# Expert lookups in float16 on VectorE alone, shared phase products, and the gathered rows of the first layer moved behind its U products

## The chip, the cores and the metric

The kernel runs on one core of a Trainium2 chip. The metric is the device time of one execution in microseconds; of the kernel before, three runs gave 2900.38, 2909.81 and 2911.41 us (median 2909.81). A difference is measured between runs of both kernels on one chip.

The engines are named as the profile names them: PE multiplies matrices (PEld is its weight load), DVE is VectorE, ACT is ScalarE, POOL is GpSimd, SP is SyncE, which here only issues DMAs. Each engine works through its own list of instructions in order.

## The reference, cut to what matters

Two layers over 256 latent tokens and 256 context tokens, 1024 features wide. Layer 0 mixes tokens with a gated MLP, layer 1 with a diagonal state-space scan; each is followed by an expert network that looks its experts up by two half keys. Only the latent tokens are given out. The lookup, for each token and each of 8 heads:

```
s_half, i_half = lax.top_k(s, 16)                 # best 16 of 128 keys, for each half
cand = s_half[:, :, 0, :, None] + s_half[:, :, 1, None, :]
top_s, top_c = lax.top_k(cand.reshape(..., 256), 16)
k1 = take_along_axis(i_half[:, :, 0], top_c // 16)   # the lookup of the first half
k2 = take_along_axis(i_half[:, :, 1], top_c % 16)    # and of the second
ids = k1 * 128 + k2
g = softmax(top_s)
act = gelu(einsum("nd,nhkd->nhk", hb, u_tab[ids]))
out = einsum("nhk,nhkd->nd", g * act, v_tab[ids])
```

The scan of layer 1 needs, for each of its states, the powers 1, z, z^2, ... of a rotation z (64 of them, as real and imaginary parts). The program calls them phases.

## The kernel before, in words

**The expert network, dense for most tokens.** For 384 of layer 0's 512 tokens (the latent ones and half of the context) and for layer 1's 256 tokens the kernel doesn't fetch experts by row: it multiplies all tokens with all 16384 experts, in 128 blocks of 128, and weights the products with a gate matrix that is zero where a token did not pick the expert. `front` (a U product) loads a block of U, splits it into a high and a low part (ACT copies `uh`, DVE subtracts to get `ul`), runs 24 matmuls and takes the gelu. `back` loads a block of V, multiplies the activations with the gates (`w`), splits both (`wh`, `wl`, `vh`, `vl`) and runs 18 matmuls (12 in layer 1) into PSUM. The first 62 (layer 0) and 66 (layer 1) U products stand ahead of the first V product; most of their activations go to DRAM and come back later (`act_d`, `actr`). The other U products stand among the V products.

**What is done beside the first U products.** The top-16 searches of the routing and the lookups (`route`, per tile of 128 tokens, in two groups of four heads each), then the gates (`gate_units`): DVE makes `eq` and two products `o` for every 8 tokens, PE multiplies them. The generators of this work are called a step at a time between the U products (`during`, `spread`). In layer 0 there are four tiles of tokens: the three dense ones and a fourth, routed first, whose 128 context tokens are the gathered ones.

**The lookup in the code before.** For each half, DVE takes the high or low four bits of the candidate's number (`pi`), casts them to float32 (`pf`), compares each with 0 to 15 (`oh`, line 504: 128 x 1024 elements, the last index being the 16 places), POOL multiplies that with the key numbers (line 506) and DVE sums over the 16 places (line 507). There are 12 groups of two halves: 8 in layer 0, 4 in layer 1.

**The gathered rows.** For the fourth tile the kernel fetches rows of U and V by index with an indirect DMA on POOL's queue (line 596), 128 + 128 of them, each 128 tokens x 1024, four buffers (`ROWS`) in turn. DVE takes a dot product with each U row (line 606, `gscr`) and adds each weighted V row to `acc` (line 619). A unit is two rows. `EARLY0` = 8 units stand among the first U products; of the rest, `MID0` = 18 units are spread over the first 56 V products and the others up to 97% of the work that follows (`cut`, `GEND`).

**The phases.** `phase_units` builds the powers for 16 groups of states at a time by doubling: with z^1 to z^k known it multiplies them by z^k. A complex product is done by 6 instructions of DVE (lines 927 to 929, three for the real and three for the imaginary part), in 6 doublings and 4 blocks: 24 times. They stand beside the first V products of layer 0.

**What sets the order.** The program is written as the generators run; then a scheduler with a model of the engines sets the order of each engine's list by that. PE's order in the V products is held as it was written (`manual_schedule`), and the gathers keep theirs. DMAs that load are issued by SP, gathers by POOL, the rest by ACT.

Of the kernel before, what the change touches and what calls it, by code (L numbers as in the profile page):

```python
# [15 lines left out]
OP = mybir.AluOpType  # L16
# [35 lines left out]
ROWS = 4  # L52
EARLY0 = 8
MID0 = 18
# [52 lines left out]
def tile_hybrid(ctx: ExitStack, tc: tile.TileContext, I, out, stop=None):  # L107
# [227 lines left out]
    def gmlp(gw, hh, hl, r, vpump, vdone, upump, mid, pump):  # L335
# [5 lines left out]
        with ExitStack() as st:  # L341
# [106 lines left out]
            with tc.issue_after(ends["out"]):  # L448
# [6 lines left out]
                   allow_small_or_imprecise_dtypes=True)  # L455
    i16 = i128[:, 0:TOPK]

# [13 lines left out]
    def route(pr, S, gates, ids, kk, big={}):  # L471
# [5 lines left out]
        for g in range(2):  # L477
            sv = pr.tile([P, HH, 2, TOPK], F32, name="sv")
            si = pr.tile([P, HH, 2, TOPK], U32, name="si")
            for h in range(HH):  # L480
# [3 lines left out]
                yield 2.5  # L484
            sf = pr.tile([P, HH, 2, TOPK], F32, name="sf")
            nc.vector.tensor_copy(sf, si)
            cand = pr.tile([P, HH, TOPK, TOPK], F32, name="cand", **big)
# [3 lines left out]
            for h in range(HH):  # L491
                scr = pr.tile([P, TOPK * TOPK], F32, name="scr2")
                top16(pr, tv[:, HH * g + h, :], ti[:, h, :], cand[:, h].rearrange("p a b -> p (a b)"), scr)
                yield 2.5
            for half in range(2):
                pi = pr.tile([P, HH, TOPK], U32, name="pi")
                if half == 0:
                    nc.vector.tensor_scalar(pi, ti, 4, None, op0=OP.logical_shift_right)
                else:
                    nc.vector.tensor_scalar(pi, ti, TOPK - 1, None, op0=OP.bitwise_and)  # L500
                pf = pr.tile([P, HH, TOPK], F32, name="pf")
                nc.vector.tensor_copy(pf, pi)
                oh = pr.tile([P, HH, TOPK, TOPK], F32, name="oh", **big)
                nc.vector.tensor_tensor(oh, pf.unsqueeze(3).to_broadcast(full),
                                        i16[:, None, None, :].to_broadcast(full), op=OP.is_equal)
                nc.gpsimd.tensor_tensor(oh, oh, sf[:, :, half, :].unsqueeze(2).to_broadcast(full), op=OP.mult)
                nc.vector.tensor_reduce(kk[half][:, HH * g:HH * g + HH], oh, axis=AX.X, op=OP.add)
                yield 2.5
        if ids is not None:
# [381 lines left out]
    def phase_units(pw):  # L891
# [21 lines left out]
        for g0 in range(0, G, n):  # L913
# [5 lines left out]
            while k < NC_ - 1:  # L919
                m = min(k, NC_ - 1 - k)  # L920
                sh = [P, n, m]
                x, y = ph[:, :, :, 1:m + 1], ph[:, :, :, k:k + 1]
                o = ph[:, :, :, k + 1:k + 1 + m]
                y0, y1 = (y[:, r].to_broadcast(sh) for r in range(2))
                t = pw.tile([P, n, NC_ // 2], F32, name="pht", tag="adasv", bufs=1)[:, :, :m]
                for r, op in ((0, OP.subtract), (1, OP.add)):
                    nc.vector.tensor_tensor(t, x[:, 1], y0 if r else y1, op=OP.mult)
                    nc.vector.tensor_tensor(o[:, r], x[:, 0], y1 if r else y0, op=OP.mult)
                    nc.vector.tensor_tensor(o[:, r], o[:, r], t, op=op)
                    yield  # L930
                k += m
# [303 lines left out]
    def spread(*items):  # L1235

        state = [[g, n, a, b, 0] for g, n, a, b in items]

        def pump(t):
            for s in state:  # L1240
                g, n, a, b, _ = s
                while s[4] < n * min((t - a) / (b - a), 1.0):
                    s[4] += next(g, None) or 1
        return pump

    def layer0():
# [53 lines left out]
        with pool("hx") as ph, pool("hold", side="right") as pk, ExitStack() as hold:  # L1300
# [57 lines left out]
            with pool("de0", 2) as pd, ExitStack() as rs:  # L1358
# [7 lines left out]
                def between():  # L1366
# [6 lines left out]
                    cut = (AHEAD0 - KEEP0) / (2 * KEYS - AHEAD0)  # L1373
                    rest.append(spread((gathers, MID0, 0.0, cut), (gathers, 128 - early - MID0, cut, GEND), (phases, 53, *PW),
                                       (ada, NQ - NS, *AW)))
# [183 lines left out]
```

## Time and profile before

| what | value |
|---|---|
| runs | 2900.38, 2909.81, 2911.41 us, median 2909.81 |
| the profiled execution's own time | 2899.56 us |
| its span (first to last instruction) | 2897.8 us, so 1.8 us lie around it |
| PE busy | 2640.4 us (91%) |
| DVE busy | 2261.9 us (78%) |
| ACT busy | 1231.5 us (42%) |
| POOL busy | 634.0 us (22%) |
| mean granted clock of PE | 0.954 |

The shares are averages over stages with different limits, so they are read by stretch of the span: how long each engine was busy in it, and for an engine that waited, on what. The first U products of layer 0 run from 484 to 835 us, its last gates to 886, its V products (with the other U products) from there to about 1745, the mixer of layer 1 to about 2035, its scores and first U products to about 2310, its V products to the end. The last column of a group of instructions is the time that its engine stood idle just before it, and who ended that. A PE clock of 1.00 is the upper of its two levels (2.4 GHz).

### The profile page before, as it was taken

The page shows a single profiled execution, that of the slowest core. Times are in us where ns is not written, and L with a number is a line of the kernel's source. Part 1 is how long each engine was busy: PE and PEld are TensorE (multiplying, and loading weights), DVE is VectorE, ACT ScalarE, POOL GpSimd, SP SyncE. Part 2 cuts the span into 40 slices and gives each one's busy share as a digit, 9 for nine tenths or more (in the row PEclk, how much of TensorE's full clock was granted, in tenths as well). Part 3 has the DMA queues.
Part 4 walks back from the last instruction along what each step waited for, and adds up shares of the span by engine and source line. Part 5 has one row for each costly group of instructions (what it writes and reads, how often), then busy time and mean ns, then how long its engine had stood idle before and what let it go on. Part 6 is the DMA issues. An engine that isn't in the chain of part 4 may idle for free.

```text
span 2897.8 us, 43990 instructions
## 1 busy us (share of the span) xinstructions
PE 2640.4 (91%) x16231; PEld 2361.3 (81%) x16231; DVE 2261.9 (78%) x4023; ACT 1231.5 (42%) x1900; POOL 634.0 (22%) x453
## 2 busy tenths in 40 slices
PE   6799978889878888999999998898889999999998
PEld 2599878788866767899999987898789988899997
DVE  7795879999997786888888876474899967755555
ACT  5453242245544322333333324334446655444443
POOL 2032122212040031355444430235300000000000
PEclk8899989999988999999999999999899999999999
DMA  8569753456668898999999978996367888866663
GB/s 273 166 218 352 264 169 116 161 174 220 219 235 277 269 350 276 316 361 345 342 343 339 340 262 277 325 336 175 126 205 267 324 279 290 275 201 214 211 202 104
DMA packets 414560, 738.76 MB, mean 255 GB/s; under 512 B 41605, under 2 KB 272261, under 8 KB 409225
## 3 DMA queue, kind: packets, MB, share of 16 engines
q1 hardware_dynamic: 310240, 507.84, 53.0%
q0 software_dynamic: 36864, 134.23, 13.1%
q10 hardware_dynamic: 67240, 93.88, 9.2%
q8 instruction: 127, 2.08, 0.3%
q14 instruction: 89, 0.72, 0.1%
HBM read 633.07 MB, written 102.77 MB: 254 GB/s over the span
## 4 chain that ended last, share of the span: by engine, by line
PE 49%; DVE 8%; DMA 6%; issue 3%; POOL 2%; ACT 1%; SPq 0%; DVEq 0%; ACTq 0%; POOLq 0%
PE bk L750 8%; PE bk L751 8%; PE bk L749 8%; PE bk L306 7%; PE bk L304 7%; PE bk L305 7%; PE bk L549 2%; DMA vr<-peer_v 1%; DVE ul L298 1%; POOL row L596 1%; DVE vl L298 1%; PE bk L1148 1%; DMA row<-peer_v,ids 1%; DMA ur<-peer_ut 1%; DMA row<-peer_u,ids 1%
## 5 line engine op out<-in xcount | busy, mean ns | idle before, releaser
L306 PE MATMUL bk<-hxh,ul 128*128 128x384 f32 (+1 forms) x2048 | 645.8, 316 | 55.0 <-DVE ul L298 54.5
L304 PE MATMUL bk<-hxh,uh 128*128 128x384 f32 (+1 forms) x2048 | 645.1, 315 | 19.4 <-ACT act L713 12.3
L305 PE MATMUL bk<-hxl,uh 128*128 128x384 f32 (+1 forms) x2048 | 640.7, 313 | 0.0
L750 PE MATMUL bk<-vl,wh 128*128 128x512 f32 x1280 | 507.6, 397 | 25.1 <-DVE vl L298 25.1
L749 PE MATMUL bk<-vh,wh 128*128 128x512 f32 x1280 | 506.8, 396 | 20.0 <-ACT wh L296 10.1
L296 ACT ACTIVATE uh<-ur 128x1024 fp32r<-128x1024 f32 x256 | 271.4, 1061 | 551.1 <-PE bk L305 490.9
L751 PE MATMUL bk<-vh,wl 128*128 128x512 f32 x1280 | 505.3, 395 | 0.1
L306 PEld LDWEIGHTS bk<-hxh,ul 128*128 128x128 f32 x2048 | 394.7, 193 | 64.3 <-DVE ul L298 63.7
L298 DVE TENSOR_TENSOR ul<-ur,uh 128x1024 fp32r<-128x1024 f32 x256 | 328.3, 1282 | 130.7 <-ACT uh L296 130.2
L304 PEld LDWEIGHTS bk<-hxh,uh 128*128 128x128 f32 x2048 | 395.6, 193 | 29.3 <-ACT act L713 16.5
L305 PEld LDWEIGHTS bk<-hxl,uh 128*128 128x128 f32 x2048 | 395.2, 193 | 5.1
L298 DVE TENSOR_TENSOR vl<-vr,vh 128x1024 fp32r<-128x1024 f32 x256 | 312.9, 1223 | 34.1 <-ACT vh L296 25.5
L296 ACT ACTIVATE wh<-w 128x384 fp32r<-128x384 f32 (+1 forms) x256 | 120.6, 471 | 509.0 <-PE bk L750 488.0
L750 PEld LDWEIGHTS bk<-vl,wh 128*128 128x128 f32 x1280 | 244.8, 191 | 77.8 <-DVE vl L298 31.7
L749 PEld LDWEIGHTS bk<-vh,wh 128*128 128x128 f32 x1280 | 244.7, 191 | 70.8 <-ACT vh L296 12.4
L296 ACT ACTIVATE vh<-vr 128x1024 fp32r<-128x1024 f32 x256 | 267.7, 1046 | 56.5 <-DMA vr<-peer_v 44.5
L751 PEld LDWEIGHTS bk<-vh,wl 128*128 128x128 f32 x1280 | 244.4, 191 | 52.1 <-DVE wl L298 1.1
L298 DVE TENSOR_TENSOR wl<-w,wh 128x384 fp32r<-128x384 f32 (+1 forms) x256 | 125.3, 490 | 165.0 <-ACT wh L296 164.5
L596 POOL DMA_INDIRECT row<-peer_v,ids x128 | 172.4, 1347 | 191.2 <-DVE acc L619 143.9
L596 POOL DMA_INDIRECT row<-peer_u,ids x128 | 163.1, 1274 | 210.6 <-DVE gscr L606 128.4
L218 DVE SCALAR_TENSOR_TENSOR adasv<-adatv,cB 128x1024 f16<-128x1024 f32 x112 | 151.3, 1351 | 58.6 <-DMA adatv<-ada_t 57.6
L619 DVE SCALAR_TENSOR_TENSOR acc<-row,wts,acc 128x1024 f32<-128x1024 f32 x127 | 162.6, 1281 | 16.3 <-DMA row<-peer_v,ids 15.5
(323 smaller groups left out, 4532.5 us busy)
## 6 DMA issues: line engine op xcount, KB each, us to landing
ur<-peer_ut SPq DMA_DIRECT2D x256, 512.0 KB, 4.4
vr<-peer_v SPq DMA_DIRECT2D x256, 512.0 KB, 4.8
gd<-Gs ACTq DMA_DIRECT2D x40, 1024.0 KB, 6.0
adatv<-ada_t SPq DMA_DIRECT2D x72, 512.0 KB, 6.1
wqT<-peer_w_q SPq DMA_DIRECT2D x64, 512.0 KB, 6.6
Gr<-gd SPq DMA_DIRECT2D x120, 192.0 KB, 6.8
wp<-wpo ACTq DMA_DIRECT2D x32, 512.0 KB, 10.3
wpi<-wp SPq DMA_DIRECT2D x16, 1024.0 KB, 6.1
```

The source lines that it names most:

```text
L218: e.scalar_tensor_tensor(scr, w, 1.0, cB[:, t], op0=OP.mult, op1=OP.mult, accum_out=mod[:, i, f, t:t + 1])
L296: nc.scalar.activation(hi, src, AF.Copy)
L298: return e.tensor_tensor(lo, src, hi.bitcast(F32), op=OP.subtract)
L304: nc.tensor.matmul(o, ah, bh, start=(i == 0), stop=False)
L305: nc.tensor.matmul(o, ah, bl, start=False, stop=False)
L306: last = nc.tensor.matmul(o, al, bh, start=False, stop=(i == n - 1))
L549: nc.tensor.matmul(pm[:, d * P:(d + 1) * P], ws[b][:, ds], kT[:, b], start=(b == 0), stop=(b == 1))
L596: tc.keep_in_program_order(nc.gpsimd.indirect_dma_start(out=r[:], out_offset=None, in_=I[f"peer_{table}{i}"], in_offset=bass.IndirectOffse ...
L619: nc.vector.scalar_tensor_tensor(acc, r, w, acc, op0=OP.mult, op1=OP.add)
L749: nc.tensor.matmul(o, wh[:, js], vh[:, qs], start=first, stop=False)
L750: nc.tensor.matmul(o, wh[:, js], vl[:, qs], start=False, stop=False)
L751: nc.tensor.matmul(o, wl[:, js], vh[:, qs], start=False, stop=last)
```

## The change

Three things are changed.

1. **Lookups.** The two halves are done together: one `pi` and one `pf` tile hold both (256 and 128 elements a partition become one cast of 128), `oh` is a float16 tile of 128 x 2048 and the numbers 0 to 15 stand in float16 (`i16`). One DVE instruction compares (line 505 of the new code), one multiplies with the key numbers, now also float16 (line 509, on DVE; POOL has no part in it any more), and two sum the halves (line 511).
2. **Phases.** The four products of a complex product are done by two instructions, each over the real and the imaginary part (lines 929 and 930), and the two sums as before (line 932): 4 instructions for 6, over the same number of elements. The temporary tile has two buffers, of the tag that the `ada` weights and the skip weights use.
3. **Gathered rows.** `EARLY0` is 0: no unit of the gathers stands beside the first U products, and the spread that runs up to `GEND` has 110 units for 102. `MID0` stays 18.

```diff
-EARLY0 = 8
+EARLY0 = 0
...
-    i16 = i128[:, 0:TOPK]
+    i16 = cp.tile([P, TOPK], F16, name="i16")
+    nc.vector.tensor_copy(i16, i128[:, 0:TOPK])
...
-            sf = pr.tile([P, HH, 2, TOPK], F32, name="sf")
-            nc.vector.tensor_copy(sf, si)
+            sf = pr.tile([P, 2, HH, TOPK], F16, name="sf")
+            nc.vector.tensor_copy(sf.rearrange("p k h t -> p h k t"), si)
...
+            pi = pr.tile([P, 2, HH * TOPK], U32, name="pi")
+            tf = ti.rearrange("p h t -> p (h t)")
+            nc.vector.tensor_scalar(pi[:, 0], tf, 4, None, op0=OP.logical_shift_right)
+            nc.vector.tensor_scalar(pi[:, 1], tf, TOPK - 1, None, op0=OP.bitwise_and)
+            pf = pr.tile([P, 2 * HH * TOPK], F16, name="pf")
+            nc.vector.tensor_copy(pf, pi.rearrange("p k n -> p (k n)"))
+            oh = pr.tile([P, 2 * HH * TOPK, TOPK], F16, name="oh", **big)
+            flat = [P, 2 * HH * TOPK, TOPK]
+            nc.vector.tensor_tensor(oh, pf.unsqueeze(2).to_broadcast(flat), i16.unsqueeze(1).to_broadcast(flat), op=OP.is_equal)
+            yield 2.5
+            both = [P, 2 * HH, TOPK, TOPK]
+            oh = oh.rearrange("p (x t) c -> p x t c", t=TOPK)
+            nc.vector.tensor_tensor(oh, oh, sf.rearrange("p k h t -> p (k h) t").unsqueeze(2).to_broadcast(both), op=OP.mult)
             for half in range(2):
-                pi = pr.tile([P, HH, TOPK], U32, name="pi")
-                if half == 0:
-                    nc.vector.tensor_scalar(pi, ti, 4, None, op0=OP.logical_shift_right)
-                else:
-                    nc.vector.tensor_scalar(pi, ti, TOPK - 1, None, op0=OP.bitwise_and)
-                pf = pr.tile([P, HH, TOPK], F32, name="pf")
-                nc.vector.tensor_copy(pf, pi)
-                oh = pr.tile([P, HH, TOPK, TOPK], F32, name="oh", **big)
-                nc.vector.tensor_tensor(oh, pf.unsqueeze(3).to_broadcast(full),
-                                        i16[:, None, None, :].to_broadcast(full), op=OP.is_equal)
-                nc.gpsimd.tensor_tensor(oh, oh, sf[:, :, half, :].unsqueeze(2).to_broadcast(full), op=OP.mult)
-                nc.vector.tensor_reduce(kk[half][:, HH * g:HH * g + HH], oh, axis=AX.X, op=OP.add)
-                yield 2.5
+                nc.vector.tensor_reduce(kk[half][:, HH * g:HH * g + HH], oh[:, half * HH:(half + 1) * HH], axis=AX.X, op=OP.add)
+            yield 2.5
...
-                y0, y1 = (y[:, r].to_broadcast(sh) for r in range(2))
-                t = pw.tile([P, n, NC_ // 2], F32, name="pht", tag="adasv", bufs=1)[:, :, :m]
+                t = pw.tile([P, 2, n, NC_ // 2], F32, name="pht", tag="adatv")[:, :, :, :m]
+                nc.vector.tensor_tensor(t, x[:, 1:2].to_broadcast(sh), y[:, ::-1].to_broadcast(sh), op=OP.mult)
+                nc.vector.tensor_tensor(o, x[:, 0:1].to_broadcast(sh), y.to_broadcast(sh), op=OP.mult)
                 for r, op in ((0, OP.subtract), (1, OP.add)):
-                    nc.vector.tensor_tensor(t, x[:, 1], y0 if r else y1, op=OP.mult)
-                    nc.vector.tensor_tensor(o[:, r], x[:, 0], y1 if r else y0, op=OP.mult)
-                    nc.vector.tensor_tensor(o[:, r], o[:, r], t, op=op)
-                    yield
+                    nc.vector.tensor_tensor(o[:, r], o[:, r], t[:, r], op=op)
+                yield
```

The scheduler's orders before and behind the two stretches of first U products are nearly the same; within them the lists shift. DVE's list at one lookup among the first U products of layer 0, before (`oh` is the comparison, `k` the sum, `ul` the low part that a U product waits for; the rest are searches and the softmax of another tile):

```order
L502 CAST pf<-pi 128x64
L515 TENSOR_REDUCE sm<-te 128x8
L468 MAX sv<-scr 128x8
L504 TENSOR_TENSOR oh<-pf,i_91 128x1024
...
L298 TENSOR_TENSOR ul<-ur,uh 128x1024
L517 TENSOR_TENSOR gates_3135<-te,sm 128x128
L467 MATCH_REPLACE scr<-sv,S_3156 128x128
L468 MAX sv<-scr 128x8
L507 TENSOR_REDUCE k_3136<-oh 128x64
L469 MAX_INDEX si<-sv,scr 128x8
L504 TENSOR_TENSOR oh<-pf,i_91 128x1024
```

and at the same lookup now:

```order
L502 CAST pf<-pi 128x128
L469 MAX sv<-scr 128x8
L519 TENSOR_REDUCE sm<-te 128x8
L505 TENSOR_TENSOR oh<-pf,i_93 128x2048
L470 MAX_INDEX si<-sv,scr 128x8
L520 RECIPROCAL sm<-sm 128x8
L298 TENSOR_TENSOR ul<-ur,uh 128x1024
L509 TENSOR_TENSOR oh<-oh,sf 128x2048
L468 MATCH_REPLACE scr<-sv,S_3158 128x128
L521 TENSOR_TENSOR gates_3137<-te,sm 128x128
L511 TENSOR_REDUCE k_3138<-oh 128x64
L511 TENSOR_REDUCE k_3139<-oh 128x64
```

Each comparison stood apart from its sum, with POOL's product between them; now comparison, product and both sums are all on DVE's list. POOL's list from the scores to the start of the V products of layer 0, before:

```order
L298 TENSOR_TENSOR wpl<-wpi,wph 128x512 x21
L506 TENSOR_TENSOR oh<-oh,sf 128x1024 x4
L596 DMA row<-peer_u,ids 128x1024 x2
L506 TENSOR_TENSOR oh<-oh,sf 128x1024 x2
L596 DMA row<-peer_u,ids 128x1024 x2
...
L596 DMA row<-peer_u,ids 128x1024 x2
L907 TENSOR_TENSOR rt<-rot 128x128
```

and now:

```order
L298 TENSOR_TENSOR wpl<-wpi,wph 128x512 x21
L600 DMA row<-peer_u,ids 128x1024 x2
L911 TENSOR_TENSOR rt<-rot 128x128
L912 TENSOR_TENSOR rt<-rot 128x64
L919 MEMSET ph 128x16
```

Sixteen products of layer 0 and the 16 early gathers have left POOL's list there; two gathers that belong to the V products have been put ahead of the phases.

## Rows read from the trace of the kernel before

**Rows 1.** Busy time of each engine by stretch, as the heading row says.

```profile
core 0: us, PE busy (x) PEld busy (x) DVE busy (x) ACT busy (x) POOL busy (x), PEclk, DMA share, GB/s
365.00:484.00 119.00, 102.31 (x800) 100.69 (x800) 100.71 (x283) 42.83 (x102) 36.92 (x23) 0.90 0.44 145
484.00:835.00 351.00, 305.29 (x1974) 289.98 (x1973) 338.52 (x897) 159.31 (x201) 67.39 (x44) 0.93 0.57 196
835.00:886.00 51.00, 28.64 (x270) 24.65 (x269) 47.54 (x63) 29.93 (x36) 11.64 (x8) 0.77 0.60 224
886.00:1142.00 256.00, 220.85 (x925) 177.37 (x923) 191.99 (x359) 81.61 (x108) 38.47 (x41) 0.94 0.88 299
1142.00:1709.00 567.00, 566.38 (x2849) 513.87 (x2849) 478.02 (x592) 198.31 (x278) 271.17 (x204) 1.00 0.95 334
2095.00:2310.00 215.00, 196.56 (x1728) 190.22 (x1727) 204.56 (x408) 127.63 (x171) 15.24 (x6) 0.97 0.76 260
```

**Rows 2.** PE's groups, 484 to 886 us: count, busy, mean ns, idle before.

```profile
L306 PE MATMUL bk<-hxh,ul 128*128 128x384 f32 x496 | 173.3, 351 | 37.1 <-DVE ul L298 36.8
L659 PE MATMUL bk<-o,eq 128*128 128x128 f16 x373 | 55.9, 235 | 18.1 <-DVE o L675 18.1
```

**Rows 3.** DVE's groups, 484 to 886 us, in the same columns.

```profile
L298 DVE TENSOR_TENSOR ul<-ur,uh 128x1024 fp32r<-128x1024 f32 x64 | 85.8, 1341 | 0.6 <-ACT uh L296 0.6
L671 DVE TENSOR_TENSOR eq<-iot,kt 128x2048 f16<-128x2048 f16 x48 | 62.8, 1328 | 1.8 <-PE bk L660 1.7
...
L606 DVE SCALAR_TENSOR_TENSOR gscr<-row,hn 128x1024 f16<-128x1024 f32 x16 | 19.4, 1210 | 6.9 <-DMA row<-peer_u,ids 6.9
L504 DVE TENSOR_TENSOR oh<-pf,i 128x1024 f32<-128x1024 f32 x14 | 16.9, 1209 | 0.0
L507 DVE TENSOR_REDUCE k<-oh 128x64 f32<-128x1024 f32 x14 | 16.9, 1207 | 5.3 <-POOL oh L506 5.3
...
L488 DVE TENSOR_TENSOR cand<-sv 128x1024 f32<-128x1024 f32 x7 | 9.4, 1336 | 0.0
L502 DVE CAST pf<-pi 128x64 f32<-128x64 uint32 x14 | 6.8, 483 | 0.0
...
L517 DVE TENSOR_TENSOR gates<-te,sm 128x128 f32<-128x128 f32 x4 | 3.2, 806 | 0.0
```

**Rows 4.** The timeline at 510 us: start, duration, instruction.

```profile
509.94 2.40 POOL L506 TENSOR_TENSOR oh<-oh,sf 128x1024 f32<-128x1024 f32 x1 [31.71 <-DVE pi L500]
510.08 3.33 DVE L298 TENSOR_TENSOR ul<-ur,uh 128x1024 fp32r<-128x1024 f32 x1
```

**Rows 5.** Single lines over the span: shortest/median/longest ns, first and last start.

```profile
L298 DVE TENSOR_TENSOR ul<-ur,uh x256: 1193/1222/3341, 488.1 to 2849.8; 128x1024 fp32r<-128x1024 f32 x128
...
L671 DVE TENSOR_TENSOR eq<-iot,kt x80: 1197/1215/3333, 606.5 to 2334.1; 128x2048 f16<-128x2048 f16 x80
...
L502 DVE CAST pf<-pi x24: 176/184/2306, 466.5 to 2250.6; 128x64 f32<-128x64 uint32 x24
...
L517 DVE TENSOR_TENSOR gates<-te,sm x6: 273/286/2383, 514.2 to 2250.9; 128x128 f32<-128x128 f32 x6
```

**Rows 6.** Layer 1, 2095 to 2310 us: groups of DVE and PE.

```profile
L298 DVE TENSOR_TENSOR ul<-ur,uh 128x1024 fp32r<-128x1024 f32 x56 | 76.0, 1358 | 9.0 <-ACT uh L296 8.9
...
L306 PE MATMUL bk<-hxh,ul 128*128 128x256 f32 x447 | 131.0, 295 | 9.4 <-DVE ul L298 9.2
```

**Rows 7.** DVE's groups of the phases by shape, 886 to 1142 us.

```profile
L927 DVE TENSOR_TENSOR pht<-ph 128x496 f32<-128x496 f32 x8 | 5.3, 668 | 0.0
...
L927 DVE TENSOR_TENSOR pht<-ph 128x16 f32<-128x16 f32 x8 | 1.6, 198 | 1.6 <-POOL ph L917 1.3
```

**Rows 8.** Gathers alone: stretch, POOL busy (count), PE clock, DMA share, GB/s.

```profile
886.00:1142.00 256.00, 37.20 (x32) 0.94 0.88 299
1142.00:1640.00 498.00, 230.98 (x175) 1.00 0.96 339
1640.00:1709.00 69.00, 40.19 (x30) 1.00 0.87 300
```

More of the change, by code (lines that the diff above doesn't have):

```diff
@@ L920, in phase_units @@
                 m = min(k, NC_ - 1 - k)
-                sh = [P, n, m]
+                sh = [P, 2, n, m]
                 x, y = ph[:, :, :, 1:m + 1], ph[:, :, :, k:k + 1]
                 o = ph[:, :, :, k + 1:k + 1 + m]
-                y0, y1 = (y[:, r].to_broadcast(sh) for r in range(2))
-                t = pw.tile([P, n, NC_ // 2], F32, name="pht", tag="adasv", bufs=1)[:, :, :m]
+                t = pw.tile([P, 2, n, NC_ // 2], F32, name="pht", tag="adatv")[:, :, :, :m]
+                nc.vector.tensor_tensor(t, x[:, 1:2].to_broadcast(sh), y[:, ::-1].to_broadcast(sh), op=OP.mult)
+                nc.vector.tensor_tensor(o, x[:, 0:1].to_broadcast(sh), y.to_broadcast(sh), op=OP.mult)
                 for r, op in ((0, OP.subtract), (1, OP.add)):
-                    nc.vector.tensor_tensor(t, x[:, 1], y0 if r else y1, op=OP.mult)
-                    nc.vector.tensor_tensor(o[:, r], x[:, 0], y1 if r else y0, op=OP.mult)
-                    nc.vector.tensor_tensor(o[:, r], o[:, r], t, op=op)
-                    yield
+                    nc.vector.tensor_tensor(o[:, r], o[:, r], t[:, r], op=op)
+                yield
                 k += m
@@ L1373, in between @@
                     cut = (AHEAD0 - KEEP0) / (2 * KEYS - AHEAD0)
-                    rest.append(spread((gathers, MID0, 0.0, cut), (gathers, 128 - early - MID0, cut, GEND), (phases, 53, *PW),
+                    rest.append(spread((gathers, MID0, 0.0, cut), (gathers, 128 - early - MID0, cut, GEND), (phases, 29, *PW),
                                        (ada, NQ - NS, *AW)))
```

## The prediction

> **What bounds the kernel now.** I read the busy times by stretch first, to see which engine is full where; then, for each stretch that the change touches, the groups of the full engine and the groups of the one that waits for it.
>
> Beside the first U products of layer 0 (484 to 835 us) DVE is busy 338.52 of 351 us and PE 305.29 [rows 1]. PE's largest wait there is for `ul`, which DVE makes: 36.8 us before the third matmul of a U product, and 18.1 us more for the gates' products `o` [rows 2]. So this stretch runs at DVE's pace. The gates of the last tile (835 to 886) are DVE's too, 47.54 of 51 us, but they hold neither lookups nor, but for two dots, rows. Among the V products it is the other way round: from 1142 to 1709 us PE is busy 566.38 of 567 us at the full clock and DVE 478.02; ahead of that, from 886 to 1142, no engine is full (PE 220.85 and DVE 191.99 of 256) and the DMA engines carry 299 GB/s at a share of 0.88. Layer 1's U products, 2095 to 2310, look like layer 0's, but closer together: DVE 204.56 and PE 196.56 of 215 [rows 1]. A microsecond of DVE is thus worth most in 484 to 835, and nearly nothing from 1142 to 1709; the change takes DVE work out of the first and puts part of it into the second.
>
> DVE loses time there in a way that its own instructions don't explain. At 510 us POOL begins its product of the lookup, and the `ul` that DVE begins 0.14 us later takes 3.33 us and ends after it [rows 4], where the median `ul` takes 1.222 us [rows 5]. The means of the stretch hold 14 such products: 64 `ul` at 1.341 for 1.222 us (7.6 us in all), 48 `eq` at 1.328 for 1.215 (5.4), 14 `pf` at 0.483 for 0.184 (4.2), 4 `gates` at 0.806 for 0.286 (2.1), and 7 `cand` at 1.336, where `oh` of the same 1024 float32 elements takes 1.209 (0.9) [rows 3, 5]. That is 20.2 us in which DVE stood still inside an instruction while POOL worked.
>
> **The change, part by part.**
>
> *Gathers leave the first U products.* 16 dots at 1.210 us are 19.4 us, and DVE waited 6.9 us for their rows [rows 3]: 26.3 us less in 484 to 886.
>
> *POOL's products go.* The 20.2 us of standing still, and 5.3 us in which the sum waited for POOL [rows 3]: 25.5 us less. After that no two-input work of POOL is left in the stretch.
>
> *The lookup itself.* For a pair of halves DVE paid two `oh` at 1.209 and two `pf` at 0.184 us, 2.79 us [rows 3, 5]; `pi` and the sums stay, with the same number of elements. Now it is one comparison and one product of 2048 float16 elements each, and a cast of 128. The nearest rows: `eq`, 2048 float16 elements in 1.215 us [rows 5], but its operands are laid out so that two neighbours always differ; and the float32 `oh`, 2 x 1.209 = 2.42 us for 2048, less one fixed cost of 0.18 (below) = 2.24. Each of the two new instructions lies between. The comparison keeps the layout of the float32 `oh`, one operand being the same element 16 times over, so I take 2.24 for it; in the product both operands run through 16 neighbours as in `eq`, so 1.215. With 0.2 for the cast this is 3.66 us, 0.87 more than before a pair; ends 2.63 (0.16 less) and 4.68 (1.9 more). Seven pairs lie in the stretch: +6.1 us, from -1.1 to +13.3.
>
> No run here shows what a repeated element does to a float16 comparison. The Trainium skill, Vector Engine (DVE) Microarchitecture Reference, 5.1 Performance modes, says that a two-source instruction with 2-byte operands, one of which is one element read 16 times, was measured to run at one element a cycle, while a row read again and again keeps two. That speaks against the comparison's gain and for the product's; were the rule wrong for the comparison, the seven pairs would come to -1.1 us in place of +6.1.
>
> *Sum for the stretch.* -26.3 - 25.5 + 6.1 = -45.7 us of DVE, of which about 12 was idle time. DVE's busy time falls from 338.5 to about 305 (338.5 - 19.4 - 20.2 + 6.1). PE has 305.3 there, so from here on both are late in turn. PE's share can shrink: its matmuls take 351 ns there [rows 2] at a clock of 0.93, and it would need about 290 us if they came at a clock of 1.00. Layer 1's stretch shows what two nearly full engines reach in lists like these: DVE 95% of the time [rows 1]. 305 us at 95% is 321 us, a gain of 30; with no idle time it is 46. I take 35, and 20 and 46 as ends.
>
> *Scores, 365 to 484 us.* Neither engine is full [rows 1]; one pair lies here. -1, between 0 and -4.
>
> *Layer 1.* 56 `ul` at 1.358 for 1.222 us are 7.6 us of standing still [rows 5, 6]; three pairs there cost 2.6 more. PE waits 9.4 us for `ul` [rows 6]. -4, between 0 and -9.
>
> *Phases.* An instruction over 496 elements takes 668 ns and one over 16 takes 198 [rows 7], so 0.98 ns an element and 182 ns fixed. The elements stay, 48 of 144 instructions go: 48 x 0.18 = 8.7 us of DVE. They lie from 886 to 1142, where DVE is full only at times: -3, between 0 and -8.7. The temporary tile now takes its turn with the skip weights' buffers; POOL finishes with those first, and I cost that at nothing (were it late, up to some 5 us).
>
> *Gathers among the V products.* All 16 rows come back there. From 886 to 1142 the 32 gathers [rows 8] become 36 (18 units of two; four of those had been issued ahead of 886): 4 rows more in a stretch where transfers are busy. From 1142 on, 205 gathers in 567 us become 220, one in 2.58 us for one in 2.77. Queued behind a gather on POOL is only the next one; on DVE the dot that waits for its row stands ahead of `vl` and `w`, and PE waits for these. What hides it: PE is full there and DVE has 89 us to spare, of which the 16 dots and sums take 20; the last 30 gathers came in 69 us, one in 2.3 us, so the chain of buffer, gather and dot can go faster than it does [rows 1, 8]. I take +4 us; if nothing hides it, 16 rows at 2.77 us are +44, and the lower end is 0.
>
> *Sum.* -35 - 1 - 4 - 3 + 4 = -39 us. From the profiled execution's 2899.6 us that is 2861. The runs lie in two pairs, 2899.6 (the profiled one) and 2900.4, and 2909.8 and 2911.4; the changed kernel's may fall at either, so I start from 2905, the middle, and predict 2866 us. 0.5% (14.5 us) is about what a measurement of this kernel can tell from no change.
>
> **The rivals.**
>
> *A, both engines follow (12%).* The U products lose all 46 us, layer 1 its 9, the phases 6, and the gathers are hidden: -61, 2844 us. For it: the idle time that goes was caused by what goes. Against it: PE's 305 us.
>
> *B, PE becomes the bound (13%).* The stretch ends at 335 us, since gates and U products come in bursts on PE too, a gain of 16; with the other terms' 4 it is 20: 2885 us. For it: PE's 87% now and 91% in layer 1 [rows 1].
>
> *C, the moved rows are paid where they go (10%).* 16 rows at the 2.3 us of the last stretch, 37 us in place of 4: -6, 2899 us, no change. For it: the DMA share is 0.95 at 334 GB/s already [rows 1], and 15 rows more of 0.5 MB are some 8 MB in those 567 us, 14 GB/s. Against it: PE is not kept waiting there by anything now.
>
> *D, slower (5%).* The chain from a free buffer over gather, landing and dot sets the pace of the V products. If every row needs the 498/175 = 2.85 us that the rows of 1142 to 1640 took [rows 8], 220 rows are 627 us for 567, +60 against a gain of 43 elsewhere: 2922 us. It decides from 2.77 us a row on, (567 + 43)/220, which is today's pace. Against it: today's pace is PE's, since PE is full, and the 2.3 us of the last stretch.
>
> That the change doesn't do what it says could only be the float16 comparison and product both at one element a cycle; that is within the ends above.
>
> **How the numbers follow.** My forecast has 60%, A 12%, B 13%, C 10%, D 5%. Faster by over 0.5%: the forecast, A, B and a third of C, 88%. Within 0.5%: the rest of C, 7%. Slower: D, 5%. The range reaches up to between B and C and down past A: 2838 to 2894. It leaves out most of C, and D.
>
> **What would show it.** In the profile of the changed kernel: the first U products end some 35 us earlier with DVE still above 95% and PE above 92% busy; the longest `ul`, `eq` and `pf` there fall from over 2.2 us to near their medians; the comparison takes 2.2 us and the product 1.2; the products of the phases come 48 times for 96 and the sums stay 48; PE stays full from about 1100 us to the end of the gathers, with a gather each 2.6 us. I am wrong if DVE falls below 90% in the U products without PE being full (something else is late, an ACT copy or a load of U), or if PE shows waits for `vl` or `w` of over 20 us among layer 0's V products that it did not have.

## The result, and the profile after

The changed kernel takes 2872.3 us (median of 4 runs, 2869.8 to 2873.9); the kernel before, beside it, 2905.1 (2896.7 to 2911.4). The ratio is 0.9889, with a 95% interval from 0.9874 to 0.9904: 32.8 us faster, where 39 had been forecast. The profiled execution of the changed kernel took 2873.9 us with a span of 2872.1; that of before took 2899.6, at the low end of its runs, so between the two traces only 25.7 us of span can be accounted for.

Busy time by stretch after, in the columns of [rows 1]:

```profile
480.00:792.00 312.00, 295.56 (x1975) 284.74 (x1975) 306.63 (x851) 158.28 (x199) 15.22 (x21) 0.97 0.58 200
792.00:840.00 48.00, 28.88 (x260) 24.12 (x259) 46.27 (x66) 31.61 (x36) 1.07 (x1) 0.75 0.46 179
840.00:1098.00 258.00, 222.79 (x922) 176.26 (x923) 185.81 (x324) 81.35 (x108) 38.78 (x41) 0.94 0.87 296
1098.00:1666.00 568.00, 562.86 (x2811) 507.97 (x2810) 475.13 (x591) 198.49 (x276) 265.65 (x200) 1.00 0.94 332
1666.00:1740.00 74.00, 54.98 (x223) 43.06 (x221) 53.01 (x78) 19.24 (x29) 26.01 (x23) 0.83 0.75 263
2069.00:2290.00 221.00, 201.67 (x1761) 195.90 (x1762) 209.90 (x434) 130.97 (x174) 0.00 (x0) 0.94 0.78 260
```

The first U products shrank from 351 to 312 us, with the same matmuls in them (1974 and 1975) and DVE at 306.63 of 312 us, 98%. The main stretch of the V products did not shrink: 568 us for 567, with 200 gathers in it where 205 stood before [rows 8]. And there is a row with no counterpart before, 1666 to 1740, where PE is at 54.98 of 74 us and gathers still run; the prediction's sign that PE stays full to the end of the gathers did not come true.

DVE's groups over 480 to 841 us, in the columns of [rows 3]:

```profile
L298 DVE TENSOR_TENSOR ul<-ur,uh 128x1024 fp32r<-128x1024 f32 x64 | 78.4, 1228 | 3.4 <-ACT uh L296 2.9 <-issue 0.4
...
L675 DVE TENSOR_TENSOR eq<-iot,kt 128x2048 f16<-128x2048 f16 x48 | 57.3, 1218 | 2.3 <-PE bk L664 1.3 <-ACT kt L643 1.0
L511 DVE TENSOR_REDUCE k<-oh 128x64 f32<-128x1024 f16 x14 | 16.4, 1213 | 0.0
L505 DVE TENSOR_TENSOR oh<-pf,i 128x2048 f16<-128x2048 f16 x7 | 16.0, 2282 | 0.0
...
L509 DVE TENSOR_TENSOR oh<-oh,sf 128x2048 f16<-128x2048 f16 x7 | 8.5, 1218 | 0.0
```

The mean `ul` is 1.228 us where it was 1.341, the mean `eq` 1.218 where it was 1.328 [rows 3]; the dots are gone, and the sums wait for nothing. The comparison is 2.282 us and the product 1.218. PE's groups there, against [rows 2]:

```profile
L306 PE MATMUL bk<-hxh,ul 128*128 128x384 f32 x496 | 168.0, 341 | 3.6 <-DVE ul L298 3.6
L663 PE MATMUL bk<-o,eq 128*128 128x128 f16 x370 | 56.4, 236 | 16.9 <-DVE o L679 14.9 <-ACT Gs L665 1.9
```

PE's wait for `ul` fell from 36.8 to 3.6 us.

The gathers alone, against [rows 8]: 200 in 568 us are one in 2.84 us (before, 205 in 567 were one in 2.77), and 21 are left for the next 74 us:

```profile
1098.00:1666.00 568.00, 265.65 (x200) 1.00 0.94 332
1666.00:1740.00 74.00, 24.65 (x21) 0.83 0.75 263
```

Laid beside the trace of before, the changed kernel's lead at eight points (us; negative is earlier) shows where time was won and given back. A `vl` is the low part of a block of V, which DVE makes for each V product; the next mixer is layer 1's, taken at the norm it starts with; `eq` is the last comparison of layer 1's gates. The last two lines are kernels of the experiments below:

| lead at | first `ul` | first `vl` | 21st `vl` | 56th `vl` | 120th `vl` | next mixer | layer 1's last `eq` | end |
|---|---|---|---|---|---|---|---|---|
| after | -4.1 | -44.5 | -32.2 | -36.7 | -33.0 | -19.0 | -29.1 | -25.7 |
| after, profiled again | -3.0 | -43.4 | -33.0 | -33.8 | -29.1 | -15.9 | -31.2 | -27.6 |
| after with the old phases | +0.4 | -38.1 | -41.2 | -40.9 | -36.3 | -25.5 | -39.4 | -35.5 |
| before with the new phases | +0.9 | +0.4 | +8.4 | +8.3 | +9.4 | +8.7 | +20.8 | +18.2 |

Some 40 us are won up to the first V product, 12 given back among the first 21 V products, 14 at the end of the V products, and 10 won in layer 1.

### The profile page after: what moved, and what is told of

The parts are those of the page before. It is cut to its first block, busy times and chain, and to the rows that moved or that the text cites. A ratio compares the mean times of both kernels' runs of the same rounds, so it can differ in the third digit from the quotient of the medians.

```text
span 2872.1 us, 43897 instructions
## 1 busy us (share of the span) xinstructions
PE 2640.3 (92%) x16231; PEld 2360.2 (82%) x16231; DVE 2233.4 (78%) x3964; ACT 1233.6 (43%) x1900; POOL 562.6 (20%) x429
## 4 chain that ended last, share of the span: by engine, by line
PE 51%; DMA 8%; DVE 7%; issue 3%; ACT 1%; POOL 1%; SPq 0%; ACTq 0%; DVEq 0%; POOLq 0%
PE bk L754 8%; PE bk L306 8%; PE bk L755 8%; PE bk L304 8%; PE bk L753 8%; PE bk L305 8%; DMA vr<-peer_v 2%; PE bk L553 1%; DMA row<-peer_v,ids 1%; DVE vl L298 1%; DMA ph_d<-ph 1%; DVE ul L298 1%; DMA actr<-act_d 1%; DMA wp<-wpo 1%; PE bk L1151 1%
## 5 line engine op out<-in xcount | busy, mean ns | idle before, releaser
L754 PE MATMUL bk<-vl,wh 128*128 128x512 f32 x1280 | 510.4, 399 | 26.0 <-DVE vl L298 24.5
L298 DVE TENSOR_TENSOR ul<-ur,uh 128x1024 fp32r<-128x1024 f32 x256 | 313.0, 1223 | 136.0 <-ACT uh L296 134.6
L753 PEld LDWEIGHTS bk<-vh,wh 128*128 128x128 f32 x1280 | 244.9, 191 | 77.5 <-ACT vh L296 20.8
L600 POOL DMA_INDIRECT row<-peer_u,ids x128 | 169.3, 1323 | 274.7 <-DVE gscr L610 166.7
L600 POOL DMA_INDIRECT row<-peer_v,ids x128 | 163.8, 1280 | 239.0 <-DVE acc L623 162.2
L623 DVE SCALAR_TENSOR_TENSOR acc<-row,wts,acc 128x1024 f32<-128x1024 f32 x127 | 162.6, 1281 | 13.3 <-DMA row<-peer_v,ids 12.7
```

The source lines that it names most:

```text
L298: return e.tensor_tensor(lo, src, hi.bitcast(F32), op=OP.subtract)
L600: tc.keep_in_program_order(nc.gpsimd.indirect_dma_start(out=r[:], out_offset=None, in_=I[f"peer_{table}{i}"], in_offset=bass.IndirectOffse ...
L623: nc.vector.scalar_tensor_tensor(acc, r, w, acc, op0=OP.mult, op1=OP.add)
L753: nc.tensor.matmul(o, wh[:, js], vh[:, qs], start=first, stop=False)
L754: nc.tensor.matmul(o, wh[:, js], vl[:, qs], start=False, stop=False)
```

## The experiments

Four questions: what won the 40 us in front (that DVE no longer stands still while POOL multiplies, which the expectations call the lock, or the gathers, or the number format); whether the 14 us at the tail are the moved rows; what the phases do; and whether the rows can be put where they cost less. Each time is a median of 4 to 12 executions. The kernel before had a median of 2902.1 us beside the first four kernels, 2903.3 beside the next four and 2906.4 beside the last four, so between groups the ratios are the better measure.

### The changed kernel again

> The changed kernel once more, beside the others on one chip, to compare them with: 2868 to 2876 us.

2872.9 us (2870.4 to 2876.9), ratio 0.9898 (0.9876 to 0.9920). The result repeats.

### Eight units of gathers back beside the first U products

```diff
-EARLY0 = 0
+EARLY0 = 8
```

> The changed kernel with the 8 early units of gathers back beside the first U products (EARLY0 = 8), lookups and phases as changed. Tail theory (the gathers have a pace of their own, some 2.8 us a row, so the 16 moved rows came out at the end of layer 0's V products and are paid there): the stretch of the first U products is 19 to 27 us longer than in the changed kernel, and the leads lost behind it (8 us up to the 56th V product, 4 to the 120th, 14 from there to the mixer of layer 1) come back almost whole: time within 8 us of the changed kernel's, 2868 to 2880 us. If the back is longer for another reason (the phases' tile, the scheduler's order), the lost leads stay and the kernel is 20 us or more slower than the changed one, 2890 us or more.

2878.0 us (2871.6 to 2883.6), ratio 0.9910 (0.9887 to 0.9933). The tail's loss is gone: the lead is 4.0 us at the 120th `vl` and 5.8 at the mixer. But the front's gain is halved. Up to the 62nd `ul` the lead is 41.8 us, and at the first `vl` 19.5. The 16 dots themselves stand early among the U products (524 to 567 us); what comes out late is the last lookup, behind the U products. PE's wait for its sums `k` between the 62nd `ul` and the first `vl` (total, times, longest us), here and then in the changed kernel:

```profile
PE bk L641 <- DVE k L511: 21.8, 2, 21.2
```

```profile
PE bk L641 <- DVE k L511: 4.5, 2, 3.9
```

So the rows are paid where they stand: as I read it, the DVE time that they take early is missing at the last lookup. In time of the whole kernel the move away from there is worth only 5.1 us: of the 22 us in front, 17 are paid elsewhere.

### More rows in the first part of the V products

```diff
-MID0 = 18
+MID0 = 26
```

> The changed kernel with MID0 = 26: the 8 units that left the first U products go beside the first 56 V products, and behind these there are 102 units as in the kernel before. Tail theory: the last gather is again some 35 us ahead of the last V product, the 14 us lost from the 120th V product to the mixer come back; the first 56 V products pay 0 to 12 us: 2855 to 2870 us. Transfer theory (8 MB more among the V products are paid wherever they stand, and dearest where the DMA engines are fullest): 0 to 10 us slower than the changed kernel, 2872 to 2882 us.

2888.5 us (2882.8 to 2892.8), ratio 0.9950 (0.9932 to 0.9968): 16 us slower than the changed kernel, and above both expected ranges. Again the tail's loss is gone (lead 4.6 at the 120th `vl`, 6.4 at the mixer), but the lead shrinks from 39.9 at the first `vl` to 10.5 at the 56th. The view that only the tail costs, and that the rows would be free elsewhere, fails; that the rows are paid in the place they are moved to holds in direction, and they cost more than it said. Whether the transfers are the reason was not tested.

### The kernel before without its early gathers

```diff
-EARLY0 = 8
+EARLY0 = 0
```

> The kernel before with EARLY0 = 0 alone. Tail theory: the first U products are 20 to 27 us shorter (16 dots of 1.2 us and the waits for their rows), the V products 15 to 25 us longer: within 8 us of the kernel before, 2897 to 2910 us. If the moved rows were hidden among the V products as predicted, 20 us or more faster: 2885 us or less.

2901.0 us (2896.8 to 2906.7), ratio 0.9992 (0.9979 to 1.0005): nothing. The front gains 22.4 us from first `ul` to first `vl`; 12 of the lead go between the 120th `vl` and the mixer, and the rest in layer 1. By itself the move of the gathers, over half of the DVE sum in the prediction, is worth no time. POOL's products are still there, and the mean `ul` is 1.413 us, from 484 to 870 us:

```profile
L298 DVE TENSOR_TENSOR ul<-ur,uh 128x1024 fp32r<-128x1024 f32 x64 | 90.4, 1413 | 4.0 <-ACT uh L296 4.0
```

### Float32 lookups, their product on DVE

Gathers and phases are as in the changed kernel. The lookups are written half by half in float32, as before; in them only the product's engine differs.

```diff
-nc.gpsimd.tensor_tensor(oh, oh, sf[:, :, half, :].unsqueeze(2).to_broadcast(full), op=OP.mult)
+nc.vector.tensor_tensor(oh, oh, sf[:, :, half, :].unsqueeze(2).to_broadcast(full), op=OP.mult)
```

> The changed kernel with the lookups in float32 half by half as before, but the product on DVE. A pair of halves then costs DVE 2 x (1.21 + 1.21 + 0.18) = 5.2 us for 3.7 in float16. Lock theory (most of the lookups' gain is that POOL's product no longer blocks DVE): 1.5 us x 7 pairs longer in layer 0's first U products and 6 us in layer 1's, 2880 to 2889 us, that is less than half of the lookups' gain gone. If the gain is float16's own: it is gone, 2890 us or more.

2886.0 us (2883.2 to 2890.6), ratio 0.9947 (0.9934 to 0.9960), within what the lock asked for. DVE's groups from 484 to 860 us:

```profile
L298 DVE TENSOR_TENSOR ul<-ur,uh 128x1024 fp32r<-128x1024 f32 x64 | 77.6, 1213 | 4.8 <-ACT uh L296 4.7
...
L506 DVE TENSOR_TENSOR oh<-oh,sf 128x1024 f32<-128x1024 f32 x14 | 17.0, 1213 | 0.0
```

`ul` is at its undisturbed length as soon as POOL's product is gone (1.413 us in the kernel above, 1.213 here), although DVE now does 17.0 us more work of its own. What is left to the changed kernel, 13 us (by the ratios 14), is the float16 form with its joined halves.

### Float16 lookups, their product on POOL

```diff
-nc.vector.tensor_tensor(oh, oh, sf.rearrange(...).unsqueeze(2).to_broadcast(both), op=OP.mult)
+nc.gpsimd.tensor_tensor(oh, oh, sf.rearrange(...).unsqueeze(2).to_broadcast(both), op=OP.mult)
```

> The changed kernel with the float16 product of the lookups on POOL instead of DVE. Lock theory: POOL's product of 2048 elements takes some 4.8 us and blocks the DVE instruction with two inputs that starts beside it, 2.5 to 4 us a pair, against 1.2 us of DVE saved: 15 to 30 us slower than the changed kernel, 2888 to 2903 us, and ul, eq or pf of over 4 us in the trace. If POOL's work does not cost DVE anything: 1.2 x 12 = 14 us of DVE less, 2860 to 2868 us.

2900.8 us (2894.4 to 2915.2), ratio 0.9996 (0.9983 to 1.0009): the whole gain of the change is gone. DVE's groups from 484 to 872 us, and the product's line over the span (shortest, median and longest ns):

```profile
L298 DVE TENSOR_TENSOR ul<-ur,uh 128x1024 fp32r<-128x1024 f32 x64 | 93.4, 1460 | 5.6 <-ACT uh L296 5.5
L679 DVE TENSOR_TENSOR o<-eq,gt 128x1024 f16<-128x1024 f16 x96 | 68.0, 758 | 0.0
...
L509 POOL TENSOR_TENSOR oh<-oh,sf x12: 4074/5012/8776, 474.9 to 2243.8; 128x2048 f16<-128x2048 f16 x12
```

`ul` is at 1.460 us, and `o` at 758 ns where the changed kernel has 686. Adding up what DVE's instructions lasted beyond their median while such a product ran gives 24.2 us (`ul` 13.5, `o` 7.3, `gates` 3.4), where DVE was spared 8.5 us of products. So with the product on POOL the number format gains nothing. The gain is that POOL's two-input product leaves; the format then makes it cheap on DVE.

### The changed kernel with the old phases

```diff
-nc.vector.tensor_tensor(t, x[:, 1:2].to_broadcast(sh), y[:, ::-1].to_broadcast(sh), op=OP.mult)
-nc.vector.tensor_tensor(o, x[:, 0:1].to_broadcast(sh), y.to_broadcast(sh), op=OP.mult)
 for r, op in ((0, OP.subtract), (1, OP.add)):
-    nc.vector.tensor_tensor(o[:, r], o[:, r], t[:, r], op=op)
+    nc.vector.tensor_tensor(t, x[:, 1], y0 if r else y1, op=OP.mult)
+    nc.vector.tensor_tensor(o[:, r], x[:, 0], y1 if r else y0, op=OP.mult)
+    nc.vector.tensor_tensor(o[:, r], o[:, r], t, op=op)
...
-(phases, 29, *PW)
+(phases, 53, *PW)
```

The temporary tile goes back to its old tag too. The number in `(phases, ...)` is that of the units which the spread hands out: the change had made them 29 for 53, one unit a complex product for two.

> The changed kernel with the phases as before (6 instructions a complex product, 53 units), lookups and gathers as changed. Density theory (the shared products need fewer units, the scheduler packs the same work beside the first 21 V products instead of the first 31, and PE waits there for vl, w and wh): the lead at the first V product stays 40 to 45 us, of which 8 to 13 us are no longer lost by the 21st V product; 2859 to 2868 us, faster than the changed kernel's 2872.9. As predicted (phases are worth 3 us): 2873 to 2879 us. If the loss there is the moved rows': no change, 2870 to 2876 us, with the lead at the 21st V product as in the changed kernel.

2860.5 us (2856.6 to 2864.1), ratio 0.9850 (0.9835 to 0.9864): 12.3 us faster than the changed kernel run again (by the two ratios 14). The new phases, which take 48 instructions off DVE, cost time, with their tile and their units.

### The kernel before with the new phases

The same edit the other way round, in the kernel before.

> The kernel before with the phases' new products alone. Density theory: the first 21 V products take 8 to 13 us longer than in the kernel before, of which some comes back by the 56th: 2905 to 2914 us beside 2902. As predicted: 0 to 9 us faster, 2893 to 2902 us.

2916.7 us (2909.2 to 2919.3), ratio 1.0038 (1.0025 to 1.0050): 13.4 us slower (by the ratio 11). At the 21st `vl` the new phases are 9.0 and 8.4 us behind the old ones (table above); in the first pair they had been 6.4 ahead at the first `vl`, so this stretch itself takes 15.4 us longer there. At the next mixer it is 6.5 (9.6 in the second profile) and 8.7 us. In the second pair another 9.5 us are lost in layer 1, whose products the edit does not touch; no run explains these. The stretches from the first `vl` to the 21st and on to the 56th, in the columns of [rows 1], first in the kernel before:

```profile
895.70:998.30 102.60, 89.05 (x372) 71.36 (x370) 80.68 (x180) 33.65 (x46) 6.68 (x12) 0.95 0.84 271
998.30:1175.00 176.70, 155.10 (x628) 123.49 (x629) 132.15 (x211) 52.37 (x70) 37.81 (x34) 0.94 0.90 308
```

and then with the new phases:

```profile
896.10:1006.70 110.60, 90.86 (x372) 70.60 (x370) 92.55 (x186) 33.84 (x45) 18.12 (x22) 0.97 0.87 285
1006.70:1183.30 176.60, 154.77 (x629) 121.00 (x629) 116.34 (x157) 52.83 (x71) 29.67 (x25) 0.96 0.87 295
```

DVE's work up to the 56th V product fell from 212.8 to 208.9 us. But the order of its instructions is drawn anew: the phases now end at about the 22nd V product (119.7 us after the first `vl`, 159.4 before, at about the 31st), and 13 dots stand in the first stretch for 10. That stretch holds 11.9 us more of DVE and lasts 8.0 longer; the next holds 15.8 us less and lasts as long as ever. More rows are gathered in the first stretch too. POOL's gathers alone, in the columns of [rows 8], from the first `vl` to the 21st: the kernel before, the same with the new phases, and the changed kernel with `MID0` = 26:

```profile
895.70:998.30 102.60, 5.77 (x6) 0.95 0.84 271
```

```profile
896.10:1006.70 110.60, 17.02 (x13) 0.97 0.87 285
```

```profile
855.80:982.00 126.20, 24.94 (x21) 0.91 0.88 300
```

Over all thirteen kernels the length of the stretch goes with the number of rows in it: 99.6 to 104.0 us with 6 (five kernels), 109.2 and 110.0 with 12, 109.7 to 116.6 with 13 or 14, 126.2 with 21. The last differs from the changed kernel (14 rows, 113.1 and 115.0 us) in the place of the rows alone, so a row does cost time there: 7 rows 11 to 13 us, by which the 7 or 8 rows drawn forward come to some 11 to 15 us (an estimate), for the 8.0 and 15.4 lost. But the next stretch, with 25 gathers for 31 in the second pair, gives nothing back. ACT's copies in the first stretch show who waits, in the kernel before:

```profile
L296 ACT ACTIVATE wh<-w 128x384 fp32r<-128x384 f32 x23 | 12.1, 524 | 51.0 <-PE bk L750 41.1 <-DVE w L734 7.0 <-PE bk L751 2.9
```

and with the new phases:

```profile
L296 ACT ACTIVATE wh<-w 128x384 fp32r<-128x384 f32 x23 | 12.0, 523 | 50.8 <-PE bk L750 33.4 <-DVE w L734 17.3
```

The wait for DVE's `w` is 10.3 us longer: `w` stands behind phases and dots in DVE's order. So I took it that packing the phases closer costs time, and spread them out again.

### The new phases spread over more V products, and the old ones at that setting

```diff
-PW = (0.0, 0.1)
-AW = (0.12, 0.35)
+PW = (0.0, 0.16)
+AW = (0.17, 0.4)
```

The second pair of lines is the window of the rows of `ada` weights, which follows the phases.

> The changed kernel with its new phases spread over more of the V products: PW = (0, 0.16) for (0, 0.1), and the ada rows behind them at AW = (0.17, 0.4) for (0.12, 0.35); the phases then stand beside the first 27 V products for the first 21. Density theory: at most half of the 8 to 13 us lost up to the 21st V product is still lost there: 2860 to 2867 us. If the new products lose by themselves (longer instructions ahead of vl, or the wait for POOL's copy at the start of each block): no change, 2869 to 2877 us.

> The control to it: the kernel with the old phases, lookups and gathers as changed, with the same PW = (0, 0.16) and AW = (0.17, 0.4). Its phases stand where they stood, beside the first 31 V products. No change from the old phases at the narrow setting: 2856 to 2865 us. If moving the ada rows matters by itself, 5 us or more from 2860.5 either way.

The new phases took 2887.3 us (2883.7 to 2887.6), ratio 0.9933 (0.9919 to 0.9946); the old ones 2874.8 (2870.6 to 2878.0), ratio 0.9894 (0.9878 to 0.9910). Both lose 14 us by the setting (by the ratios 10 and 13; which of its two windows costs that was not separated), so the new phases are above both expected ranges, and the control did move. The new phases lose 12.5 to the old ones here as they lose 12.3 at the narrow setting. Yet here both end at about the same time (156 and 162 us after the first `vl`), with 12 rows gathered up to the 21st `vl` in both. Neither packing nor the rows drawn forward is therefore the whole cause. The loss has moved too: up to the 21st `vl` both take the same time (109.1 and 109.9 us), and it falls on the stretch from there to the 56th, with 26 rows in both. Old phases:

```profile
969.40:1140.10 170.70, 155.00 (x636) 122.31 (x634) 123.61 (x206) 53.59 (x73) 29.41 (x29) 0.96 0.87 298
```

New phases:

```profile
962.40:1150.60 188.20, 160.50 (x629) 126.17 (x629) 119.05 (x184) 52.76 (x72) 31.15 (x29) 0.92 0.81 276
```

The waits of SP's queue, which issues the loads, in the same stretch (total, times and longest us), with the old phases:

```profile
SPq L129 <- DVE vl L298: 50.6, 25, 5.4
SPq L129 <- DVE w L738: 20.5, 15, 5.5
```

and with the new ones:

```profile
SPq L129 <- DVE w L738: 49.1, 15, 7.5
SPq L129 <- DVE vl L298: 33.4, 26, 4.7
```

The loads stand 28.6 us longer for DVE's `w` and 17.2 shorter for `vl`, the transfers fall from 298 to 276 GB/s, and the stretch is 17.5 us longer with 4.6 us less work on DVE. The amount of DVE's work, the number of rows and full transfers can't explain that. What is left is the order in which DVE, ACT and SP wait for each other; that is a reading of these rows, and no kernel tested it by itself. Which property of the new phases would upset the order (longer instructions ahead of `w`, the temporary tile that shares its buffers with the loads of `ada` weights, or the copy on POOL that they wait for, 4.9 us in place of 1.3 in the pair above) is open.

### Five row buffers, with the old phases

```diff
-ROWS = 4
+ROWS = 5
```

> Old phases, lookups and gathers as changed, five buffers for gathered rows instead of four. Tail theory: the gathers are behind because a row holds a buffer for four times the pace; with five the chip can go faster, and DVE's list has 254 for 249 of the 256 row instructions ahead of the last vl: the 11 us lost from the 120th V product to the mixer become 3 to 7: 2852 to 2858 us. If the buffers don't set the pace (DVE's list does): less than 3 us, 2858 to 2863 us.

2859.7 us (2854.6 to 2861.1), ratio 0.9836 (0.9823 to 0.9850), against 2860.5 with four. The last gather starts 20 us earlier than with four, but the lead still falls from 36.5 at the 120th `vl` to 28.3 at the mixer. By the ratios it is 4 us less, which the two intervals don't keep apart. Buffers set little of the time, if any.

### Four units of gathers early, with the old phases

```diff
-EARLY0 = 0
+EARLY0 = 4
```

> Old phases, lookups as changed, EARLY0 = 4: half of the moved rows back beside the first U products. If the move is worth what the first U products gain less the tail: these are 10 to 13 us longer, the tail 5 to 9 us shorter, 2861 to 2868 us. If the moved rows were hidden behind: 2870 us or more. If the tail costs more than the front gives: under 2858 us.

2871.5 us (2870.7 to 2873.8), ratio 0.9882 (0.9867 to 0.9897): 11 us slower than with none early (by the ratios 9). By the time alone that falls to "hidden behind", but the trace shows them half hidden: the front loses 10.9 of its 38.5 us, as expected, and the tail's loss falls from 10.8 to 6.9, by 3.9 where 5 to 9 were expected.

The best kernels run are the changed one with the old phases, with four or five row buffers: 2860.5 and 2859.7 us, 0.4% faster than the changed kernel and 1.5% to 1.6% faster than the one before.

## Why the prediction was right, and which of its terms were not

The time came out 6 us above the forecast, inside its range and with its likeliest case. Term by term, at the points of the table:

**First U products: right, and a little more.** -35 was taken, between -20 and -46; the trace shows 40.4 us from first `ul` to first `vl`. DVE's busy time was to fall to about 305 us and is 306.63. The choice between 95% and 100% of DVE was mis-sized: it is at 98% of 312 us, with PE at 95%, so the two lists fit better than layer 1's did. The working by steps holds as well. The 20.2 us of standing still are gone (about 1 us is left from 480 to 841 beside POOL's instructions, among them the two-input products of the rotation, which the prediction overlooked); the kernel with float32 lookups shows that taking POOL's product away frees `ul` though the lookup stays in float32, and the one with the float16 product on POOL that putting it back costs everything. Of the 40 us, the lookups are 18 (early gathers kept) and the gathers 22 (lookups kept), though after the lookups alone the U products themselves run 40 us shorter and the last lookup then comes late behind them. In time of the whole kernel the split is another: the gathers' move brings nothing in the old kernel and 5 us behind the lookups, while the lookups with the new phases bring 24 without it.

**The lookup: right.** 2.24 us were taken for the comparison and 1.215 for the product, and 2.282 and 1.218 came out. The nearest row for the comparison was the one of the float32 lookups, whose layout stayed. The layout is what tells it from `eq`, a float16 comparison of as many elements in 1.218 us. The rule of the Trainium skill, Vector Engine (DVE) Microarchitecture Reference, 5.1 Performance modes, that one element read 16 times takes a two-source float16 operation down to one element a cycle while a repeated row keeps two, agrees with both numbers: 2048 elements each, and 1.064 us between them.

**Scores: within the noise of one execution.** -1 was taken; the first `ul` leads by 4.1 and 3.0 us in two profiles, and is 0.4 late with the same lookups and the old phases.

**Layer 1: mis-sized.** -4 was taken, with -9 as the end. From the norm behind layer 1's mixer (leads of 18.6 and 14.5 us) to the last `eq` 10.5 us were won, 16.7 in the second profile. The terms were the right ones (the `ul` that stood still), but I counted the 7.6 us of `ul` alone; over all of DVE's instructions that ran beside POOL's products there, the trace of before has 13.3 us. Some 3.5 us of it are given back by the end in both profiles.

**Phases: the step that failed.** "-3, between 0 and -8.7", from 48 fixed costs saved, with the buffer's wait "at nothing". It is +11 to +14, in two pairs of kernels and again at a third setting. The saving is there: the lines of the phases keep DVE busy for 38.7 us where they took 47.7, 9.0 less for the 8.7 forecast. But DVE was never the bound of that stretch, as [rows 1] had it: DVE 191.99 of 256 us. I priced the instructions and not what else moves with them. Up to the 21st `vl` it is in large part the 13 or 14 gathered rows for 6; at the wide setting the same loss comes without that, and its cause stays open, the order in which the engines wait for each other being the reading that is left. The rows gave no size for this, and an end above nothing was missing.

**Gathers among the V products: mis-sized, and the mechanism wrong.** +4 was taken because 220 gathers would come one in 2.58 us under a full PE. They did not speed up: one in 2.84 us. In DVE's order three rows stand to a V product as before, so the 16 moved rows come last and outlive the V products. After the last `vl` the sums of the last rows stand among the additions that write the experts' output back to the tokens (`XT`), and PE's transposes for these (L586) wait; DVE there, from 1719 us on:

```profile
1719.01 1.23 DVE L298 TENSOR_TENSOR vl<-vr,vh 128x1024 fp32r<-128x1024 f32 x1 [4.79 <-ACT vh L296]
1720.15 5.24 DVE L623 SCALAR_TENSOR_TENSOR acc<-row,wts,acc 128x1024 f32<-128x1024 f32 x4
1727.21 1.28 DVE L623 SCALAR_TENSOR_TENSOR acc<-row,wts,acc 128x1024 f32<-128x1024 f32 x1 [1.82 <-DMA row<-peer_v,ids]
1728.41 2.15 DVE L328 SCALAR_TENSOR_TENSOR XT<-bk,mod,XT 128x128 f32<-128x128 f32 x8
```

Before, the last sum was at 1716.2 us and six `vl` came after it. PE's waits from 1650 to 1757 us (total, times, longest) are where the 14 us show:

```profile
PE bk L586 <- DVE XT L328: 6.4, 3, 4.2
PE bk L753 <- ACT vh L296: 6.3, 1, 6.3
PE bk L553 <- DMA wqT<-peer_w_q: 5.2, 2, 4.5
PE bk L754 <- DVE vl L298: 4.6, 3, 3.7
```

In the kernel before the same four, from 1690 to 1776 us, are 2.8, 0.7, 4.3 and 4.1 us. These are 10 of the 14 us. This is rival C's outcome, the moved rows paid where they go, at somewhat over a third of its price, but not by the full transfers that spoke for C: the DMA share is 0.75 at the tail. The rows were hidden as far as PE was full, and no further. That the tail's loss is the moved rows is shown: it goes with them in both kernels that put them elsewhere. That they are then paid in that other place was not in the prediction.

The errors met from both sides: first U products, scores and layer 1 came 15 us better than taken (5.4, 3.1 and 6.5), the V products from the first to the mixer 24.5 worse (25.5 for the 1 that phases and gathers were to cost), and the rest 3.8 worse. From -39 that is the -25.7 of the two traces; the medians lie 32.8 apart, since the profiled execution of before was a short one. That the total is so close is luck: the gain in front and the loss behind were both under-estimated, and partly cancel.

## What to carry to other kernels

A two-input operation on POOL can hold up a full DVE for most of its own duration; look for DVE instructions whose longest duration is far above their median while POOL works, and move the operation to DVE even where DVE is the bound. Fewer and larger instructions were no gain in a stretch where no engine is full: time the edit alone, since a bundle with a good part hides a bad one (here 12 us of 45). Work moved under a full engine is free only if its own pace fits there; ask where its last piece comes out.

## What the runs showed that I had not expected

The float16 product of 2048 elements takes 5.0 us (median) on POOL and 1.218 on DVE, and DVE loses more time to 7 of them (24.2 us) than they would take on DVE itself (8.5 us). With five row buffers for four the last gather started 20 us earlier, and the time stayed within 1 us (by the ratios 4).
